# Cache attention: three pairs of PSUM banks, latents turned three steps ahead, square sums two steps behind, another order

## The chip, the cores and the metric

The kernel runs on one core of a Trainium2 chip: TensorE (PE; its weight loads are listed as PEld), VectorE (DVE), ScalarE (ACT) and GpSimd (POOL) work side by side, each in the order of its own queue, and wait for each other by semaphores. SyncE (SP) and GpSimd issue DMAs. Data lies in SBUF; matmuls write to PSUM, which has 8 banks of 512 float32 columns on 128 partitions. The metric is device time in microseconds, the median of several executions.

## The reference

One inference step of a decoder with two layers, for a prompt (1,024 tokens) and 8 samples of 4 new tokens. Each layer has a pooling mixer, a convolution mixer and an attention with a low-rank latent; only the last is touched. For the samples it runs over 8,192 past tokens of each, held in pages of latents and rotary keys:

```
    def step(carry, pt):
        m, lsum, acc = carry
        lat = cache_latent[layer, pt]
        krp = cache_krope[layer, pt]
        kn = key_nope(lat, w_uk, kn_g)
        s = attn_scores(qn, qr, kn, krp)
        m_new = jnp.maximum(m, jnp.max(s, axis=-1))
        corr = jnp.exp(m - m_new)
        p = jnp.exp(s - m_new[..., None])
        lsum = lsum * corr + jnp.sum(p, axis=-1)
        acc = acc * corr[..., None] + jnp.einsum('bhqk,bkc->bhqc', p, lat.astype(jnp.float32))
        return (m_new, lsum, acc), None
```

`key_nope` is the root-mean-square norm of `lat @ w_uk` for each head, `attn_scores` the scaled sum of `qn` with `kn` and `qr` with `krp`. There are 4 heads, 64 key dimensions without position, 32 rotary ones, latents of 128 and 4 queries for each sample. The prompt's own causal attention and the projections are computed as well.

## The kernel before

Each layer runs through a stage of input projections, a **cache stage** (`sample_attn`, L471), a **prompt stage** (`prompt_attn`, L790) that also finishes the cache attention (`finish`, L732), and output projections. In the cache and prompt stages the order of the instructions is the order in which the code is written; the stages around them are ordered by a scheduler.

The cache stage treats the past in 16 units `u` (half a sample's pages each, 4,096 tokens), a unit in 8 steps `q`; `tau` counts all 128 steps. One step covers 4 blocks of 128 tokens:

- `T` (L509): VectorE turns the latents of a step into `lT` (three buffers). The loop calls `T(tau + 2)` at the end of step `tau`.
- `K` (L519): TensorE multiplies two blocks of `lT` with `WK`, which holds `w_uk` in 256 columns and the sample's folded queries in 16 more, into a pair of PSUM banks `kproj`; each product is two MATMUL records of 272 columns. ScalarE squares the 256 columns into `sq`. `nope` (L535): ScalarE copies the 16 score columns. There are two `K` in a step, so 8 records, and two pairs of banks (`ps2`, tag `kp`) that take turns.
- `tree` (L539): GpSimd adds the two halves of the squares (`t32`). `red` (L544): VectorE sums these to `ms`, one step behind.

What belongs to a whole unit is spread over the steps of the next one: `lnexp` (ScalarE) and `newton` (VectorE) make the reciprocal root `rs`, `scale` (GpSimd) multiplies the scores with it, `rope` (TensorE) computes the rotary part of the scores from turned rotary keys (`krT`, VectorE) into `ropesc`, `addrope` (VectorE) adds it, `colmax`, `maxT` and `bcast` find the maximum over the tokens (the PSUM tile is `pm`, the two transposes run on TensorE), `expo` subtracts it, `expo_act` (ScalarE) takes the exponential into `p`, `rowsum` (VectorE) sums, `pv` (TensorE) multiplies `p` with the latents into `po`, and `pvend` (VectorE) copies `po` to `O`. In the kernel before `krT` and `rope` stand in the unit itself, at steps 2 and 5, and 6 and 7. Three gathers fetch data with indirect DMAs that GpSimd issues: `gather_c` (latents as `T` wants them, `latc`, two units ahead, step 6), `gather_n` (latents as `pv` wants them, `lat`, step 2) and `gather_kr` (rotary keys, step 7). `ada_step` (L618) computes, in layer 0 and every second unit, modulation vectors for later (`adaps`, `adapt`; seven times).

PSUM is one pool of eight banks for the whole program: two pairs `kp`, two single banks `tr`, one `rp`, one `mi` (`psr`, `psm`; `adaps`, `po`, `pm`). `ropesc` lies in `tr`. What is left after the last unit (`tail`, L696) is a generator that the prompt stage advances between its own tiles.

Of the kernel before, what the change touches and what calls it, by code (L numbers as in the profile page):

```python
# [9 lines left out]
F32 = mybir.dt.float32  # L10
# [37 lines left out]
def _build(nc, tc, a, ctx):  # L48
# [5 lines left out]
    pp = ctx.enter_context(tc.tile_pool(name="pp", bufs=2, space=PSUM))  # L54
# [7 lines left out]

    def ps2(name):
        return pp.tile([128, 2, 512], F32, tag="kp", name=name)

    def ps1(name):
        return pp.tile([128, 512], F32, tag="tr", name=name)

    def psr(name):
        return pp.tile([128, 512], F32, tag="rp", name=name, bufs=1)  # L70

    def psm(name):
        return pp.tile([128, 512], F32, tag="mi", name=name, bufs=1)

    def f(ap):
        return ap.bitcast(F32)
# [27 lines left out]
    def sub(out, x, y, e=None):  # L104
        tt(out, x, y, ALU.subtract, e)

    def split(h, lo, src, e=None):
        s.copy(h, src)  # L108
        sub(lo, src, f(h), e)

# [360 lines left out]
    def sample_attn(l, keep, pool, warm):  # L471
# [6 lines left out]
        krs = []  # L478
# [30 lines left out]
        def T(tau):  # L509
            if tau >= NU * NSTEP:  # L510
                return
            h, q = H[tau // NSTEP], tau % NSTEP
            h.lT = getattr(h, "lT", {})
            h.lT[q] = pool.tile([128, 512], F32, tag="lT", name="lT", bufs=3)
            v.transpose(h.lT[q], h.latc[:, 512 * q:512 * q + 512])  # L515
            if q == NSTEP - 1:
                h.latc = None

        def K(h, q, j):  # L519
            if q == 0 and j == 0:  # L520
                h.nope = keep.tile([128, 32, NH, NT], F32, tag="nope", name="nope", bufs=2)
                h.ms = keep.tile([128, 32, NH], F32, tag="ms", name="ms", bufs=2)
            if j == 0:
                h.sq = pool.tile([128, 4, 256], F32, tag="sq", name="sq", bufs=2)
# [14 lines left out]
        def tree(h, q):  # L539
            sv = h.sq.rearrange("p n (h x d) -> p (n h) x d", h=NH, x=2)  # L540
            h.t32 = pool.tile([128, 16, 32], F32, tag="t32", name="t32", bufs=2)
            add(h.t32, sv[:, :, 0, :], sv[:, :, 1, :], g)

        def red(h, q):  # L544
            v.tensor_reduce(h.ms[:, 4 * q:4 * q + 4, :].rearrange("p n (h o) -> p (n h) o", o=1), h.t32, AX.X, ALU.add)  # L545
# [95 lines left out]
        T(1)  # L641
        new_wk(1)
        for i in range(2):
            v.memset(pbuf[i][:, 512:528], 0.0)
        for tau in range(NSTEP * NU):
            u, q = divmod(tau, NSTEP)
            h, pu = H[u], u - 1
            hp, hpp = H.get(pu), H.get(u - 2)
            kp = K(h, q, 0)
            nope(h, q, 0, kp)  # L650
            if tau:
                red(H[(tau - 1) // NSTEP], (tau - 1) % NSTEP)
            if hp is not None:
                if q == 1:
# [10 lines left out]
            T(tau + 2)  # L665
            if hp is not None:
                if q == 0:
                    lnexp(hp)
                elif q == 1:
                    scale(hp)  # L670
                elif q == 5:
                    maxT(hp, pu)
                elif q == 6:
                    bcast(hp, pu)
                    expo(hp, pu)
                elif q == 7:
                    expo_act(hp, pu)
            if q == 0:
                if hpp is not None:
# [3 lines left out]
            elif q == 2:  # L683
                gather_n(u)
                krT(h, 0)
            elif q == 5:
                krT(h, 1)
            elif q >= 6:
                rope(h, q - 6)
                (gather_c if q == 6 else gather_kr)(u + 2)  # L690
# [5 lines left out]
        def tail():  # L696
            u = NU - 1
            h, hp = H[u], H[u - 1]
            red(h, NSTEP - 1)
            krs.clear()  # L700
            lnexp(h)
            rowsum(hp, u - 1)
# [87 lines left out]
    def prompt_attn(l, mixM, mixA):  # L790
# [164 lines left out]
        with tc.tile_pool(name=f"sa{l}", bufs=1, reuse_waits="tile") as pool:  # L955
            sample = sample_attn(l, keep, pool, warm)
        with tc.tile_pool(name=f"pa{l}", bufs=1, reuse_waits="tile") as pool:
# [714 lines left out]
```

## Time and profile before

| | |
|---|---|
| median of 3 runs | 1657.57 us (1655.13 to 1658.05) |
| the profiled execution | 1656.43 us, its span 1654.7 us |
| TensorE busy | 1580.0 us (95%) |
| VectorE, ScalarE, GpSimd busy | 1079.6, 798.5, 745.5 us (65%, 48%, 45%) |
| costliest groups | `kproj` matmuls 525.9 us, ScalarE's `sq` 305.6 us, GpSimd's `t` 325.5 us |
| moved by DMA | 254.48 MB |

The busy time of an engine is an average over stages that have different limits, and a matmul's end is modelled, so that TensorE's share says little about how close it is to its pace. The starts of matmuls tell more. In the trace an idle time stands in brackets, with the instruction that ended it.

### The profile page before, as it was taken

The numbers are of one execution on the slowest core, as the hardware profiler recorded it, in microseconds if no ns is written. First come the engines' busy times: TensorE is split into PE (matmuls) and PEld (weight loads), VectorE is DVE, ScalarE is ACT, GpSimd is POOL, SyncE is SP. The second block draws the span as 40 slices with busy tenths as digits, with TensorE's granted clock in tenths as the row PEclk, the third lists the DMA queues.
The fourth block names the chain that finished last, engine by engine and source line by source line (L and its number), as shares of the span: only waits on it lengthen the run. The fifth ranks groups of instructions, "written<-read, shape, count | busy, mean of one in ns | idle before, by whom it ended". The sixth has DMA issues, their size and how long they took to land.

```text
span 1654.7 us, 28034 instructions
## 1 busy us (share of the span) xinstructions
PE 1580.0 (95%) x10576; PEld 1367.6 (83%) x10576; DVE 1079.6 (65%) x2131; ACT 798.5 (48%) x1935; POOL 745.5 (45%) x594
## 2 busy tenths in 40 slices
PE   4899999999999999999989999999999999999999
PEld 2799999877777777889969999997777777779999
DVE  7747754577777777783377477555777777776622
ACT  4434444355555556583245344434555555566600
POOL 3301221366666667364443012124666666665520
PEclk8999999999999999999999999999999999999999
DMA  9101331676666673214422112326565555531142
GB/s 374 54 31 63 78 65 65 204 281 271 267 264 261 266 287 154 65 45 146 174 81 68 42 57 72 77 58 238 229 230 229 228 225 226 207 116 51 54 167 79
DMA packets 79557, 254.48 MB, mean 154 GB/s; under 512 B 25472, under 2 KB 49088, under 8 KB 69184
## 3 DMA queue, kind: packets, MB, share of 16 engines
q0 software_dynamic: 13824, 151.00, 23.9%
q1 hardware_dynamic: 65600, 101.69, 18.9%
q8 instruction: 85, 1.39, 0.3%
q14 instruction: 48, 0.39, 0.1%
HBM read 231.87 MB, written 20.80 MB: 153 GB/s over the span
## 4 chain that ended last, share of the span: by engine, by line
PE 79%; DVE 9%; POOL 5%; ACT 3%; issue 3%; DMA 1%; SPq 0%; DVEq 0%; ACTq 0%; POOLq 0%
PE kproj L531 23%; POOL t L96 4%; PE ropesc L557 3%; PE po L608 3%; PE outa L188 2%; PE outa L190 2%; PE outa L186 2%; PE PTp L156 2%; ACT sq L93 2%; PE rawps L206 2%; PE rawps L204 2%; PE rawps L205 2%; PE pvo L204 1%; PE outb L190 1%; PE outb L186 1%
## 5 line engine op out<-in xcount | busy, mean ns | idle before, releaser
L531 PE MATMUL kproj<-WK,lT 128*128 128x272 f32 x2048 | 525.9, 405 | 26.1 <-DVE lT L515 16.3
L531 PEld LDWEIGHTS kproj<-WK,lT 128*128 128x128 f32 x2048 | 368.0, 190 | 151.1 <-ACT nope L537 58.8
L93 ACT ACTIVATE sq<-kproj 128x512 f32<-128x512 f32 x512 | 305.6, 597 | 305.4 <-PE kproj L531 304.6
L96 POOL TENSOR_TENSOR t<-sq 128x512 f32<-128x512 f32 x256 | 325.5, 1272 | 224.1 <-ACT nope L537 222.0
L545 DVE TENSOR_REDUCE ms<-t 128x16 f32<-128x512 f32 x256 | 173.1, 676 | 156.9 <-POOL t L96 156.6
L96 POOL TENSOR_TENSOR wt<-wraw,wt 128x1024 fp32r<-128x1024 f32 x44 | 106.9, 2432 | 313.6 <-ACT wt L108 309.5
L515 DVE STREAM_TRANSPOSE lT<-latc 128x512 f32<-128x512 f32 x256 | 179.2, 700 | 0.3 <-issue 0.3
L108 ACT CAST wt<-wraw 128x1024 fp32r<-128x1024 f32 x44 | 46.7, 1064 | 124.5 <-PE outb L190 80.1
L537 ACT COPY nope<-kproj 128x32 f32<-128x32 f32 x512 | 92.4, 180 | 0.0
L96 POOL TENSOR_TENSOR kn<-raw,ones 128x128 f32<-128x128 f32 x18 | 12.2, 676 | 163.3 <-DVE raw L96 88.2
L1342 PE MATMUL zma<-hT,wt 128*128 128x352 f32 x192 | 50.6, 368 | 25.8 <-ACT hT L1122 18.7
L557 PEld LDWEIGHTS ropesc<-BD,krT 128*128 128x128 f32 x512 | 64.8, 191 | 3.5
L557 PE MATMUL ropesc<-BD,krT 128*128 128x64 f32 x512 | 67.2, 274 | 0.0
L865 DVE TENSOR_REDUCE pmx<-sc 128x1 f32<-128x128 f32 (+3 forms) x64 | 48.0, 750 | 27.1 <-PE pvo L156 21.7
L1342 PEld LDWEIGHTS zma<-hT,wt 128*128 128x128 f32 x192 | 37.0, 215 | 32.8 <-ACT hT L1122 21.5
L608 PE MATMUL po<-lat,p 128*32 128x128 f32 x2048 | 62.5, 274 | 0.0
L608 PEld LDWEIGHTS po<-lat,p 128*32 128x32 f32 x2048 | 53.9, 110 | 10.3 <-ACT nope L537 10.0
L908 ACT CAST PT<-PTp 128x512 fp32r<-128x512 f32 (+2 forms) x96 | 42.8, 481 | 40.1 <-PE PTp L156 39.5
L96 DVE TENSOR_TENSOR PT<-PTp,PT 128x512 fp32r<-128x512 f32 (+2 forms) x96 | 50.2, 550 | 16.6 <-ACT PT L908 15.6
L96 POOL TENSOR_TENSOR qkT<-src,qkT 96x512 fp32r<-96x512 f32 x32 | 40.9, 1280 | 28.0 <-ACT qkT L811 27.6
L206 PE MATMUL rawps<-wqh,hT 128*128 128x416 f32 x144 | 50.9, 354 | 0.0
L93 ACT ACTIVATE P<-sc,pmx 128x128 f32<-128x128 f32 (+3 forms) x64 | 47.9, 748 | 6.0 <-DVE pmx L865 5.4
(452 smaller groups left out, 3828.1 us busy)
## 6 DMA issues: line engine op xcount, KB each, us to landing
wada<-in_w_ada SPq DMA_DIRECT2D x11, 2048.0 KB, 9.5
wraw<-in_w_in SPq DMA_DIRECT2D x32, 512.0 KB, 3.8
wraw<-in_w_out SPq DMA_DIRECT2D x14, 512.0 KB, 5.2
qscr<-qkm SPq DMA_DIRECT2D x32, 192.0 KB, 2.1
xo<-in_xT SPq DMA_DIRECT2D x8, 528.0 KB, 4.9
xscr<-xn SPq DMA_DIRECT2D x8, 528.0 KB, 3.0
xo<-xscr SPq DMA_DIRECT2D x8, 528.0 KB, 4.8
vscr<-Vm SPq DMA_DIRECT2D x16, 256.0 KB, 2.2
```

The lines of the kernel that those rows point to most:

```text
L93: s.activation(out, in_, func, **k)
L96: (e or v).tensor_tensor(out, x, y, op)
L186: te.matmul(outs[n], wt[:, 0, k, :], hi[:, n * CH:(n + 1) * CH], start=(k == 0), stop=False)
L190: te.matmul(outs[n], wt[:, 1, k, :], hi[:, n * CH:(n + 1) * CH], start=False, stop=(k == 7))
L206: te.matmul(out, ll, rh, start=False, stop=stop)
L515: v.transpose(h.lT[q], h.latc[:, 512 * q:512 * q + 512])
L531: te.matmul(kp[:, i, 0:KPC], lT[:, sl], wk, start=True, stop=True)
L537: s.copy(h.nope[:, t0:t0 + 2].rearrange("p n h t -> p n (h t)"), kp[:, :, 256:KPC])
L545: v.tensor_reduce(h.ms[:, 4 * q:4 * q + 4, :].rearrange("p n (h o) -> p (n h) o", o=1), h.t32, AX.X, ALU.add)
L557: te.matmul(h.pr[:, o:o + 64], h.krT[c][:, 128 * k:128 * k + 128], BD[:, h.b, :], start=True, stop=True)
L608: te.matmul(h.po[32 * j:32 * j + 32, 0:128], p[:, 16 * t:16 * t + 32], h.lat[:, t * 128:(t + 1) * 128], start=(q == 0), stop=(q == 7))
L1342: te.matmul(o, zmw[j][:, i // 2, k, :], (lo if i == 1 else hi)[:, c], start=(k == 0 and i == 0), stop=(k == 7 and i == 1))
```

## The change

- `banks(stage)` closes the PSUM pool and opens another. In the cache stage it has three pairs `kp` and no `tr` in use, in all other stages two pairs as before. `ropesc` goes from `tr` to the single bank `mi` (in the last unit to `rp`).
- `lT` has four buffers, `sq` and `t32` three (they had two), `nope` three.
- `T(tau + 3)` stands at the head of step `tau`; before, `T(tau + 2)` stood at its end.
- `red` sums the squares of two steps ago, from a list; before, of one step ago.
- The unit's work is spread anew: `krT` at steps 0 and 1 of the next unit, `newton` and `scale` at 2, `lnexp` at 1, `rope` at 2 and 3, `addrope` at 4, `colmax` at 5, `maxT` at 6, `bcast` and `expo` at 7; one unit later `expo_act` at 0, `rowsum` and `pv` at 3, `pvend` at 4. `gather_n` and `gather_c` both stand at step 5. The tail has two square sums, an exponential and two rope groups more.

```
+    def banks(stage):
+
+        psum.close()
+        pools.append((psum.enter_context(tc.tile_pool(name=f"pp{len(pools)}", bufs=1, space=PSUM, reuse_waits="tile")),
+                      {"cache": 3, "main": 2}[stage]))
...
-            h.lT[q] = pool.tile([128, 512], F32, tag="lT", name="lT", bufs=3)
+            h.lT[q] = pool.tile([128, 512], F32, tag="lT", name="lT", bufs=4)
...
+            halves.append((h, q, t32))
+
+        def red():
+            h, q, t32 = halves.pop(0)
...
-                h.pr = ps1("ropesc")
+                h.pr = (psr if h is H.get(NU - 1) else psm)("ropesc")
...
+            T(tau + 3)
             kp = K(h, q, 0)
             nope(h, q, 0, kp)
-            if tau:
-                red(H[(tau - 1) // NSTEP], (tau - 1) % NSTEP)
+            if tau > 1:
+                red()
             if hp is not None:
-                if q == 1:
+                if q < 2:
+                    krT(hp, q)
+                elif q == 2:
                     newton(hp)
-                elif q == 3:
+                elif q == 4:
                     addrope(hp)
-                elif q == 4:
+                elif q == 5:
                     colmax(hp)
-            if hpp is not None and q == 0:
-                rowsum(hpp, u - 2)
             kp = K(h, q, 1)
             tree(h, q)
             nope(h, q, 1, kp)
-            T(tau + 2)
...
+            if hpp is not None:
+                if q == 0:
+                    expo_act(hpp, u - 2)
+                elif q == 3:
+                    rowsum(hpp, u - 2)
                     for i in range(8):
                         pv(hpp, u - 2, i)
+                elif q == 4:
                     pvend(hpp, u - 2)
...
+            if q == 5:
                 gather_n(u)
+                gather_c(u + 2)
```

How the order stands at the three places that matter, in layer 1. First **TensorE**, one unit of the cache stage, from one `po` to the next, before (`kproj` rows are products, four rows of the program to a step; `pm<-ident,mx` is the transpose of the maximum, `pm<-ident,M` the broadcast):

```order
L608 MATMUL po<-lat_8_12386,p_10753 32x128 x32
L531 MATMUL kproj<-WK_90,lT 128x272 x20
L156 MATMUL pm<-ident,mx 16x128
L531 MATMUL kproj<-WK_90,lT 128x272 x4
L589 MATMUL pm<-ident,M 128x16
L557 MATMUL ropesc<-BD,krT 128x64 x4
L531 MATMUL kproj<-WK_90,lT 128x272 x4
L557 MATMUL ropesc<-BD,krT 128x64 x4
L531 MATMUL kproj<-WK_90,lT 128x272 x4
L608 MATMUL po<-lat_9_12587,p_10754 32x128 x32
```

And after:

```order
L620 MATMUL po<-lat_8_12450,p_10765 32x128 x32
L541 MATMUL kproj<-WK_90,lT 128x272 x12
L166 MATMUL pm<-ident,mx 16x128
L541 MATMUL kproj<-WK_90,lT 128x272 x4
L601 MATMUL pm<-ident,M 128x16
L541 MATMUL kproj<-WK_90,lT 128x272 x12
L569 MATMUL ropesc<-BD,krT 128x64 x4
L541 MATMUL kproj<-WK_90,lT 128x272 x4
L569 MATMUL ropesc<-BD,krT 128x64 x4
L620 MATMUL po<-lat_9_12652,p_10766 32x128 x32
```

The rows are the same ones; `po` follows the second rope group directly, and the maximum comes three steps behind `po` where it came five steps behind it.

**VectorE**, around the maximum of a unit (`lT` is a turned latent tile, `ms<-t` a square sum, `mx` the maximum per column), before:

```order
L96 TENSOR_TENSOR nope<-nope,ropesc 128x512
L515 STREAM_TRANSPOSE lT<-latc_10_12469 128x512
L545 TENSOR_REDUCE ms<-t_12805 128x16
L581 TENSOR_REDUCE mx<-nope 128x16
L515 STREAM_TRANSPOSE lT<-latc_10_12469 128x512
L545 TENSOR_REDUCE ms<-t_12823 128x16
L515 STREAM_TRANSPOSE lT<-latc_10_12469 128x512
L586 TENSOR_REDUCE M<-pm 16x1
```

And after:

```order
L104 TENSOR_TENSOR nope<-nope,ropesc 128x512
L624 COPY O<-po 128x128
L525 STREAM_TRANSPOSE lT<-latc_11_12654 128x512
L557 TENSOR_REDUCE ms<-t_12776 128x16
L593 TENSOR_REDUCE mx<-nope 128x16
L525 STREAM_TRANSPOSE lT<-latc_11_12654 128x512
L557 TENSOR_REDUCE ms<-t_12831 128x16
L598 TENSOR_REDUCE M<-pm 16x1
```

The transpose of a step now stands ahead of its square sum and its maximum, and the first transpose behind `O` is the first that reads the following unit's latents.

**GpSimd**, the gathers of a unit among its trees (`t`), before:

```order
L482 DMA lat_9_12587<-in_lat,idx_87 128x4096
L96 TENSOR_TENSOR t_12603<-sq 128x512
L96 TENSOR_TENSOR t_12621<-sq 128x512
L96 TENSOR_TENSOR t_12638<-sq 128x512
L96 TENSOR_TENSOR t_12659<-sq 128x512
L482 DMA latc_11_12671<-in_latc,idx_87 128x4096
```

And after:

```order
L104 TENSOR_TENSOR nope<-nope,rs 128x512
L104 TENSOR_TENSOR t_12574<-sq 128x512
L104 TENSOR_TENSOR t_12629<-sq 128x512
L104 TENSOR_TENSOR t_12649<-sq 128x512
L492 DMA lat_9_12652<-in_lat,idx_87 128x4096
L492 DMA latc_11_12654<-in_latc,idx_87 128x4096
```

Four trees stood between the two large gathers; now none does.

## Rows read from the trace of the kernel before

**Rows 1.** The page, part 4: shares of the chain that ended last, by engine.

```profile
PE 79%; DVE 9%; POOL 5%; ACT 3%; issue 3%; DMA 1%; SPq 0%; DVEq 0%; ACTq 0%; POOLq 0%
```

**Rows 2.** The tile `kproj`, TensorE alone, layers 0 and 1: ns min/median/max, first and last start.

```profile
L531 PE MATMUL kproj<-WK,lT x1024: 392/392/657, 319.5 to 659.7; 128*128 128x272 f32 x171
...
L531 PE MATMUL kproj<-WK,lT x1024: 392/392/661, 1131.7 to 1463.3; 128*128 128x272 f32 x171
```

**Rows 3.** Windows: us, busy time of PE, PEld, DVE, ACT, POOL, granted clock, DMA share, GB/s.

```profile
319.50:330.00 10.50, 10.45 (x36) 7.39 (x37) 5.26 (x12) 5.39 (x16) 4.45 (x4) 0.84 0.43 183
...
1200.00:1300.00 100.00, 96.26 (x714) 72.74 (x712) 76.00 (x136) 56.98 (x169) 68.45 (x59) 1.00 0.59 226
```

**Rows 4.** Timeline of TensorE, one unit of layer 1: start us, us, instruction, idle before.

```profile
1298.02 1.96 PE L608 MATMUL po<-lat,p 128*32 128x128 f32 x64
1299.90 8.12 PE L531 MATMUL kproj<-WK,lT 128*128 128x272 f32 x32
1308.34 2.07 PE L531 MATMUL kproj<-WK,lT 128*128 128x272 f32 x8 [0.32 <-DVE lT L515]
1310.40 0.28 PE L156 MATMUL pm<-ident,mx 128*16 128x128 f32 x1
1311.11 2.07 PE L531 MATMUL kproj<-WK,lT 128*128 128x272 f32 x8 [0.43 <-ACT sq L93]
1313.11 0.23 PE L589 MATMUL pm<-ident,M 16*128 16x16 f32 x1
1313.27 1.10 PE L557 MATMUL ropesc<-BD,krT 128*128 128x64 f32 x8
1314.21 2.05 PE L531 MATMUL kproj<-WK,lT 128*128 128x272 f32 x8
1316.10 1.00 PE L557 MATMUL ropesc<-BD,krT 128*128 128x64 f32 x8
1316.94 2.05 PE L531 MATMUL kproj<-WK,lT 128*128 128x272 f32 x8
1318.92 1.96 PE L608 MATMUL po<-lat,p 128*32 128x128 f32 x64
```

**Rows 5.** Timeline of TensorE, layer 0, a unit with modulation work.

```profile
435.97 1.92 PE L225 MATMUL adaps<-wada,cTt 128*32 128x512 f32 x16
437.83 2.10 PE L531 MATMUL kproj<-WK,lT 128*128 128x272 f32 x8
...
442.96 0.61 PE L156 MATMUL adapt<-ident,adamg 128*128 128x128 f32 x4
443.41 2.00 PE L531 MATMUL kproj<-WK,lT 128*128 128x272 f32 x8
445.24 1.00 PE L557 MATMUL ropesc<-BD,krT 128*128 128x64 f32 x8
```

**Rows 6.** Timeline of the weight loads (PEld), the unit of rows 4.

```profile
1301.91 1.67 PEld L531 LDWEIGHTS kproj<-WK,lT 128*128 128x128 f32 x8 [0.34 <-ACT nope L537]
1303.92 1.67 PEld L531 LDWEIGHTS kproj<-WK,lT 128*128 128x128 f32 x8 [0.34 <-ACT nope L537]
```

**Rows 7.** Timeline of ScalarE, the same unit: the first pair of one step.

```profile
1303.19 0.60 ACT L93 ACTIVATE sq<-kproj 128x512 f32<-128x512 f32 x1 [0.48 <-PE kproj L531]
1303.69 0.18 ACT L537 COPY nope<-kproj 128x32 f32<-128x32 f32 x1
```

**Rows 8.** Timeline of VectorE, the same unit, around the column maximum.

```profile
1309.32 1.03 DVE L581 TENSOR_REDUCE mx<-nope 128x16 f32<-128x512 f32 x1
1310.25 0.71 DVE L515 STREAM_TRANSPOSE lT<-latc 128x512 f32<-128x512 f32 x1
```

**Rows 9.** DMA issues (median us to landing); GpSimd's timeline; a window of two us.

```profile
latc<-in_latc,idx POOLq DMA_INDIRECT x32, 8.3
...
1315.30 0.95 POOL L482 DMA_INDIRECT latc<-in_latc,idx  x1
...
1269.00:1271.00 2.00, 1.76 (x8) 1.44 (x8) 2.00 (x6) 0.77 (x4) 1.28 (x1) 1.00 0.98 418
```

More of the change, by code (lines that the diff above doesn't have):

```diff
@@ L53, in _build @@
     big = ctx.enter_context(tc.tile_pool(name="big", bufs=8))
-    pp = ctx.enter_context(tc.tile_pool(name="pp", bufs=2, space=PSUM))
+    psum = ctx.enter_context(ExitStack())
+    pools = []
     dp = ctx.enter_context(tc.tile_pool(name="dp", bufs=1, space=DRAM))
@@ L61, in slot_r @@
         return big.tile([128, 4, TOK], F32R, tag="B", name=name)
+    def banks(stage):
+        psum.close()
+        pools.append((psum.enter_context(tc.tile_pool(name=f"pp{len(pools)}", bufs=1, space=PSUM, reuse_waits="tile")),
+                      {"cache": 3, "main": 2}[stage]))
     def ps2(name):
-        return pp.tile([128, 2, 512], F32, tag="kp", name=name)
+        pp, n = pools[-1]
+        return pp.tile([128, 2, 512], F32, tag="kp", name=name, bufs=n)
     def ps1(name):
-        return pp.tile([128, 512], F32, tag="tr", name=name)
+        return pools[-1][0].tile([128, 512], F32, tag="tr", name=name, bufs=2)
     def psr(name):
-        return pp.tile([128, 512], F32, tag="rp", name=name, bufs=1)
+        return pools[-1][0].tile([128, 512], F32, tag="rp", name=name)
     def psm(name):
-        return pp.tile([128, 512], F32, tag="mi", name=name, bufs=1)
+        return pools[-1][0].tile([128, 512], F32, tag="mi", name=name)
     def f(ap):
@@ L109, in split @@
         sub(lo, src, f(h), e)
+    banks("main")
     cpk = cp.tile([128, sum(CPK.values())], F32, name="cpk")
@@ L477, in sample_attn @@
         H = {}
-        krs = []
+        krs, halves = [], []
         def rows(u, dst, src):
@@ L520, in K @@
             if q == 0 and j == 0:
-                h.nope = keep.tile([128, 32, NH, NT], F32, tag="nope", name="nope", bufs=2)
+                h.nope = keep.tile([128, 32, NH, NT], F32, tag="nope", name="nope", bufs=3)
                 h.ms = keep.tile([128, 32, NH], F32, tag="ms", name="ms", bufs=2)
             if j == 0:
-                h.sq = pool.tile([128, 4, 256], F32, tag="sq", name="sq", bufs=2)
+                h.sq = pool.tile([128, 4, 256], F32, tag="sq", name="sq", bufs=3)
             wk = WK[h.b % 2]
@@ L540, in tree @@
             sv = h.sq.rearrange("p n (h x d) -> p (n h) x d", h=NH, x=2)
[L541 to L545, printed above, removed]
+            t32 = pool.tile([128, 16, 32], F32, tag="t32", name="t32", bufs=3)
+            add(t32, sv[:, :, 0, :], sv[:, :, 1, :], g)
+            halves.append((h, q, t32))
+        def red():
+            h, q, t32 = halves.pop(0)
+            v.tensor_reduce(h.ms[:, 4 * q:4 * q + 4, :].rearrange("p n (h o) -> p (n h) o", o=1), t32, AX.X, ALU.add)
         def krT(h, c):
@@ L641, in sample_attn @@
         T(1)
+        T(2)
         new_wk(1)
@@ L664, in sample_attn @@
             nope(h, q, 1, kp)
-            T(tau + 2)
             if hp is not None:
-                if q == 0:
+                if q == 1:
                     lnexp(hp)
-                elif q == 1:
-                    scale(hp)
-                elif q == 5:
+                elif q in (2, 3):
+                    rope(hp, q - 2)
+                    if q == 2:
+                        scale(hp)
+                elif q == 6:
                     maxT(hp, pu)
-                elif q == 6:
+                elif q == 7:
                     bcast(hp, pu)
                     expo(hp, pu)
[L676 to L679, printed above, removed]
+            if hpp is not None:
[3 more added lines that the diff above has]
+                    rowsum(hpp, u - 2)
                     for i in range(8):
                         pv(hpp, u - 2, i)
+                elif q == 4:
                     pvend(hpp, u - 2)
-            elif q == 2:
+                    hpp = None
+            if q == 5:
                 gather_n(u)
[L685 to L690, printed above, removed]
+                gather_c(u + 2)
+            elif q == 7:
+                gather_kr(u + 2)
+            if u == NU - 1 and q in (4, 6):
+                krT(h, q // 2 - 2)
             ada_step(u, q)
@@ L698, in tail @@
             h, hp = H[u], H[u - 1]
-            red(h, NSTEP - 1)
+            red()
+            red()
             krs.clear()
+            expo_act(hp, u - 1)
             lnexp(h)
+            rope(h, 0)
+            rope(h, 1)
             rowsum(hp, u - 1)
@@ L955, in prompt_attn @@
         with tc.tile_pool(name=f"sa{l}", bufs=1, reuse_waits="tile") as pool:
+            banks("cache")
             sample = sample_attn(l, keep, pool, warm)
+            banks("main")
         with tc.tile_pool(name=f"pa{l}", bufs=1, reuse_waits="tile") as pool:
```

## The prediction

> **What bounds the kernel now.** I read first the shares of the chain that ended last, then the two stretches in which the cache attention runs, then one unit of it on each engine. The chain lies on TensorE for 79% [rows 1], so a gain has to be time that TensorE stands still. The diff touches the cache stage alone, and that runs twice: its first and last key products start at 319.5 and 659.7 us, and at 1131.7 and 1463.3 us [rows 2]. That is 340.2 + 331.6 = 671.8 us of the profiled execution's own 1656.43 us (1654.7 us of it the span); the median of the runs is 1657.57, 1.14 more, and I add that at the end.
>
> In such a stretch TensorE counts as busy for 96.26 of 100 us, VectorE for 76, GpSimd for 68 and ScalarE for 57, at granted clock 1.00 [rows 3], the 2.4 GHz level. The busy figure hides the loss, because a matmul's end is modelled. Starts show it: in layer 1 one unit, from one `po` to the next, takes 1318.92 - 1298.02 = 20.90 us [rows 4]. In it stand 8 steps of 8 `kproj` matmuls. Where nothing holds them, 8 take 445.24 - 443.41 = 1.83 us [rows 5], or 1316.10 - 1314.21 = 1.89 behind a rope group [rows 4]. The four steps behind `po` start 1299.90 and the fifth 1308.34, so 2.1 us each. Two waits do this. Weight loads of plain steps stand 0.34 us until ScalarE's `nope` copy has emptied a bank pair [rows 6]: from a step's first load at 1301.91 to the end of its first pair's copy at 1303.69 + 0.18 pass 1.96 us [rows 6, 7], and with two pairs the banks are wanted again after 1.83. Later in the unit the latents are late: [rows 4] show 0.32 us on `lT` at 1308.34, and the step behind the column maximum starts 0.71 us after the `pm` transpose, since VectorE turned the next latents only at 1310.25, behind the maximum [rows 8], and ScalarE then followed late.
>
> **The change, part by part.** *Three bank pairs.* A pair is wanted again after 3 x 0.92 = 2.75 us instead of 1.83, against the 1.96 it takes; 0.8 us of room for each pair. ScalarE needs 0.60 + 0.18 us for a pair [rows 7] that comes every 0.92, and 57% of 20.90 = 11.9 us in a unit [rows 3], so it keeps up. The rsqrt and the exponential (which now stand behind the second product pair of steps 1 and 0) fit into that room. The 0.34 us wait goes; what is next late in a plain step is nothing, and it runs at TensorE's own 1.83 to 1.89 us. I take 1.86.
>
> *Latents three steps ahead, at the head of a step.* VectorE's transpose now waits only for the products of the step before the current one, and TensorE wants its result three steps on, some 5.6 us for a 0.71 us instruction. The waits at 1308.34 and 1311.11 go. Behind a waiting transpose stand, on VectorE, the square sum and the unit's own instruction. VectorE's 76% of 20.90 us is 15.9 us in a unit, less than what TensorE will need, so it stays in step.
>
> *Square sums two steps behind, three buffers of squares and halves.* VectorE no longer waits for GpSimd in the step; that wait cost nothing while TensorE was late, and now keeps VectorE ahead. Count of instructions: the same.
>
> *Order.* Key rotations, rope products and everything behind them go one to three steps later; `po` follows the second rope group directly. TensorE's own work is unchanged. A unit without modulation work is then 8 x 1.86 = 14.88, two rope groups of 0.84 and 0.94 (1.78), `po` 1.88 (1299.90 - 1298.02), the small broadcast 0.16 (1313.27 - 1313.11) and the `pm` transpose, which never stands unhindered in [rows 4], taken like the broadcast, 0.16 (bounds 0.1 and 0.71): **18.86 us, 2.0 less than 20.90**. In layer 0 seven units have also 437.83 - 435.97 = 1.86 for `adaps` and 443.41 - 442.96 = 0.45 for `adapt` [rows 5]: 21.17. `adaps` now takes the bank that `po` held until VectorE copies `O`; between stands a whole product step of 1.86 us for a copy that follows `po` at once, so nothing; without that cover some 0.5 us, 7 times.
>
> *GpSimd's gathers.* `lat` moves from step 2 to step 5 and `latc` from 6 to 5, behind each other on one queue, each an issue of 0.95 us. So the tree of that step is followed by 1.9 us of issues where TensorE's step takes 1.86; GpSimd falls back some 1.7 us and wins 0.6 per step back, and the square sums read two steps later. A gather lands 8.3 us after its issue (median of 32) [rows 9]. It is 128 x 4096 x 4 bytes = 2.10 MB; the engines moved 418 GB/s in a full stretch [rows 9], so a second one behind it takes 5.0 us more: an estimate of 13.3 us from the first issue, which is some 2.2 us after the end of the step's products (1315.30 against 1313.11 [rows 9, 4]). The first latents of the gathered unit are turned at step 5 of the next unit, 18.86 - 1.86 = 17.0 us after those products. So they land 1.5 us early, and TensorE notices only another 1.3 us later, because between that transpose and `pm` lie 2 steps (3.7 us) for 2.4 us of VectorE's work (0.7 transpose, 0.7 sum, 1.03 maximum [rows 8]). Cost nothing; the cover is 2.8 us.
>
> The Trainium skill speaks against that: its page DMA: Bandwidth & Descriptors (Where 436 GB/s comes from) states about 358 GB/s as what HBM gives one core. By it the second gather takes 5.9 us and the cover shrinks by 0.9, still above zero. The 418 GB/s of the row is above that figure, so I keep the row.
>
> *The stages' ends.* Rope of the last unit (1.78 us) goes behind the loop, where before one group of 0.84 stood behind the last products; the first scores may wait for a bank that the last products used; banks change hands per tile. Plus 1.5 us per layer; bounds 0 (the prompt's start may have gaps to take it) and 3.
>
> **The sum.** Layer 1: unit 0 is products alone, 14.88; unit 1 has rope, `pm` and broadcast, 16.98; units 2 to 14 are 13 x 18.86 = 245.2; unit 15 to its last product start, 18.5. That is 295.5, plus a slow beginning as before: in the first 10.5 us of layer 0's stage the granted clock is 0.84 and only 36 matmuls start, for which 8.2 us would do at 0.229 each [rows 3]; about 2 of it remain. 297.5 against 331.6: 34.1 less. Layer 0: 14.88 + 19.3 + 7 x 18.86 + 6 x 21.17 + 18.5 + 2 = 313.7 against 340.2: 26.5 less. Together 60.6, less 3 for the ends: 57.6. 1656.43 - 57.6 = 1598.8, and on the median **1600 us**. With 1.83 for every product step and no cost at the ends it is 1589; with 1.89, `pm` at 0.71 and 3 us at each end 1627.
>
> **The rivals.**
> *Half of the gain goes to a new wait.* VectorE's queue now holds, in steps 4 to 7, four instructions that wait for TensorE in order (the rope addition, `O`, the maximum over `pm`, the subtraction), and a late one delays the next transpose and the maximum that TensorE's `pm` needs. Today the waits that come from there are 0.32 us at 1308.34, 0.2 ahead of `pm` (1310.40 against 1308.34 + 1.83) and 0.6 behind it, 1.1 in a unit [rows 4]. If they stay, 30 units x 1.1 = 33 us: 1633. For it: VectorE will be busy 15.9 of 18.9 us. Against it: the maximum has 2.8 us of room by the count above.
>
> *The pair of gathers is late: slower.* If the two land not 13.3 but 20 us after the first issue, the transpose of step 5 waits beyond its cover by 20 - 16.1 = 3.9 us in each of units 2 to 15 of both layers, 28 x 3.9 = 109 us: 1709. From 16.1 us the gain shrinks, at some 18.2 it is gone. For it: in the trace no two such gathers are under way together. Against it: `krs` follows `latc` today by 3 us in that queue, and the stretch of [rows 9] shows the engines at 0.98 without a pause.
>
> *The change does nothing.* If the bank wait were only ScalarE's pace seen from TensorE, a third pair would fill and the wait return: 1657. ScalarE's 0.78 us for a pair against 0.92 says no. The Trainium skill has such a case, in TensorE: Matmul & The Clock Gate (HAM oscillation — how this bites in real kernels): PSUM double-buffering gave one matmul kernel no further gain, 125.5 against 126.6 us. The page puts that kernel's trouble down to waits for DMA; here [rows 6] name ScalarE's copy as what ends the wait.
>
> **How the numbers follow.** Forecast, 1588 to 1617: 0.66. Half the gain lost, to 1634: 0.17. Slower by the gathers: 0.08. Nothing: 0.05. Better than 1588: 0.04. The range 1588 to 1634 leaves out 0.17. A measurement of this kernel tells about 0.2% (3.3 us) from no change. Faster 0.87, same 0.05, slower 0.08.
>
> **What would show it.** In the changed profile: plain product steps 1.83 to 1.89 us apart with no wait for `nope` in front of their weight loads; units 18.9 us in layer 1 and 21.2 with modulation; the key products from first to last some 297 and 314 us; no wait of TensorE for `lT`; `latc` landing some 13 us after the issue of `lat`; the granted clock 1.00 as before. I am wrong if VectorE's transposes wait for `latc`, if `pm` still waits for the maximum, or if the plain steps stay at 2.0 us.

## The result, and the profile after

The changed kernel takes 1605.16 us (median of 4 runs, 1603.93 to 1606.35) against 1657.09 for the kernel before beside it: a ratio of 0.9688, interval 0.9671 to 0.9705, 3.1% faster. The forecast was 1600, its range 1588 to 1634. The profiled execution took 1606.35 us, its span is 1604.6.

The two stages are where the prediction put them. First the shares of the chain that ended last, by engine (79% on TensorE before [rows 1]); then the tile `kproj` in layers 0 and 1 (first and last start behind the comma); then 100 us of layer 1 (columns as in [rows 3]):

```profile
PE 87%; DVE 6%; DMA 2%; issue 2%; ACT 1%; POOL 1%; SPq 0%; DVEq 0%; POOLq 0%; ACTq 0%
```

```profile
L541 PE MATMUL kproj<-WK,lT x1024: 392/392/497, 320.8 to 634.5; 128*128 128x272 f32 x171
...
L541 PE MATMUL kproj<-WK,lT x1024: 392/392/497, 1111.0 to 1408.1; 128*128 128x272 f32 x171
```

```profile
1180.00:1280.00 100.00, 100.00 (x755) 82.94 (x754) 90.40 (x150) 62.10 (x187) 74.65 (x65) 1.00 0.63 253
```

The stages take 313.7 and 297.1 us (340.2 and 331.6 in [rows 2]; forecast 313.7 and 297.5), 61.0 less together. The whole profiled run gained 50.1. The missing 10.9 lie outside: 1.3 ahead of the first stage (320.8 against 319.5), 4.5 between the stages (476.5 against 472.0) and 5.1 behind the second (196.5 against 191.4). The 1.3 is no work of the change: the order there is the same, and from 140 to 150 and from 150 to 160 us the granted clock reads 0.92 and 0.91 where the trace of before has 1.00; the first key product of the traces here starts anywhere from 319.3 to 323.1 us.

One unit of layer 1 on TensorE (the window ends inside the last `po`), and, behind the dots, three steps of its weight loads, to be held against [rows 4] and [rows 6]:

```profile
1209.44 1.95 PE L620 MATMUL po<-lat,p 128*32 128x128 f32 x64
1211.33 5.77 PE L541 MATMUL kproj<-WK,lT 128*128 128x272 f32 x24
1216.93 0.27 PE L166 MATMUL pm<-ident,mx 128*16 128x128 f32 x1
1217.04 2.00 PE L541 MATMUL kproj<-WK,lT 128*128 128x272 f32 x8
1218.97 0.22 PE L601 MATMUL pm<-ident,M 16*128 16x16 f32 x1
1219.13 5.77 PE L541 MATMUL kproj<-WK,lT 128*128 128x272 f32 x24
1224.73 1.00 PE L569 MATMUL ropesc<-BD,krT 128*128 128x64 f32 x8
1225.57 2.05 PE L541 MATMUL kproj<-WK,lT 128*128 128x272 f32 x8
1227.46 1.00 PE L569 MATMUL ropesc<-BD,krT 128*128 128x64 f32 x8
1228.39 0.32 PE L620 MATMUL po<-lat,p 128*32 128x128 f32 x4
...
1219.12 5.34 PEld L541 LDWEIGHTS kproj<-WK,lT 128*128 128x128 f32 x24
```

From `po` to `po` 18.95 us: the eight steps 5.60 + 1.93 + 5.60 + 1.89 = 15.02, rope 0.84 + 0.93, `po` 1.89, `pm` 0.11, the small broadcast 0.16. No row has an idle time in front, and the loads no longer wait for `nope`.

### The profile page after: what moved, and what is told of

The parts are those of the page before. It is cut to its first block, busy times and chain, and to the rows that moved or that the text cites. A ratio compares the mean times of both kernels' runs of the same rounds, so it can differ in the third digit from the quotient of the medians.

```text
span 1604.6 us, 28029 instructions
## 1 busy us (share of the span) xinstructions
PE 1547.2 (96%) x10576; PEld 1386.7 (86%) x10576; DVE 1122.6 (70%) x2131; ACT 790.4 (49%) x1935; POOL 743.8 (46%) x594
## 4 chain that ended last, share of the span: by engine, by line
PE 87%; DVE 6%; DMA 2%; issue 2%; ACT 1%; POOL 1%; SPq 0%; DVEq 0%; POOLq 0%; ACTq 0%
PE kproj L541 29%; PE po L620 4%; PE ropesc L569 3%; PE outa L198 2%; PE outa L200 2%; PE outa L196 2%; PE PTp L166 2%; PE rawps L216 2%; PE rawps L214 2%; PE rawps L215 2%; PE pvo L214 1%; DMA src<-qscr 1%; PE outb L200 1%; PE outb L196 1%; PE outb L198 1%
## 5 line engine op out<-in xcount | busy, mean ns | idle before, releaser
L541 PE MATMUL kproj<-WK,lT 128*128 128x272 f32 x2048 | 497.5, 397 | 3.9 <-DVE lT L525 3.9
L541 PEld LDWEIGHTS kproj<-WK,lT 128*128 128x128 f32 x2048 | 378.9, 190 | 90.0 <-issue 15.9
L525 DVE STREAM_TRANSPOSE lT<-latc 128x512 f32<-128x512 f32 x256 | 177.4, 694 | 35.7 <-PE kproj L541 31.9
L557 DVE TENSOR_REDUCE ms<-t 128x16 f32<-128x512 f32 x256 | 167.0, 652 | 10.8 <-POOL t L104 10.5
L104 DVE TENSOR_TENSOR PT<-PTp,PT 128x512 fp32r<-128x512 f32 (+2 forms) x96 | 50.2, 551 | 21.8 <-ACT PT L929 20.8
L104 POOL TENSOR_TENSOR nope<-nope,rs 128x512 f32<-128x512 f32 x32 | 35.2, 1100 | 35.2 <-DVE rs L581 35.2
```

Source lines behind the costliest of these rows:

```text
L104: (e or v).tensor_tensor(out, x, y, op)
```

## The experiments

Ratios are to the kernel before, run beside each. The old order is that of the kernel before; "lag" is square sums two steps behind, "lead" latents three steps ahead.

| kernel | pairs | order | lag | lead | us | ratio, interval |
|---|---|---|---|---|---|---|
| before | 2 | old | no | no | 1657.1 | 1 |
| e_bk3 | 3 | old | no | no | 1659.7 | 1.0012, 1.0002 to 1.0021 |
| e_lag | 3 | old | yes | yes | 1647.1 | 0.993, 0.991 to 0.995 |
| e_order | 2 | new | no | no | 1675.7 | 1.0104, 1.0084 to 1.0125 |
| e_twotlate | 2 | new | yes | no | 1628.4 | 0.9827, 0.9800 to 0.9855 |
| e_two | 2 | new | yes | yes | 1628.0 | 0.9818, 0.9801 to 0.9834 |
| e_red1 | 3 | new | no | yes | 1614.1 | 0.9731, 0.9711 to 0.9751 |
| e_tlate | 3 | new | yes | no | 1607.0 | 0.9689, 0.9673 to 0.9705 |
| after | 3 | new | yes | yes | 1605.2 | 0.9688, 0.9671 to 0.9705 |

### Parts taken away from the changed kernel

Two pairs (e_two):

```diff
-                      {"cache": 3, "main": 2}[stage]))
+                      {"cache": 2, "main": 2}[stage]))
```

> The changed kernel with two pairs of banks for the key products in the cache stage instead of three (the freed banks stay empty); order, latents three steps ahead and square sums two steps behind stay. Theory 1 (two separate waits, as the prediction has it): a pair is wanted again after 1.83 us and takes 1.96, so a plain step takes 1.96 to 2.1 instead of 1.83, 8 x 0.13 to 0.27 = 1.0 to 2.2 us per unit, 32 units: 1637 to 1675, middle about 1645; weight loads wait for the nope copy again. Theory 2 (the latents alone held TensorE, the third pair only adds slack): 1604 to 1612, and the wait for nope stays away.

1628.0, between the two theories. The wait for `nope` is back in front of the weight loads. Their group in the view of lines (busy, mean ns, idle before it), in the changed kernel and in e_two:

```profile
L541 PEld LDWEIGHTS kproj<-WK,lT 128*128 128x128 f32 x2048 | 378.9, 190 | 90.0 <-issue 15.9
```

```profile
L541 PEld LDWEIGHTS kproj<-WK,lT 128*128 128x128 f32 x2048 | 367.0, 190 | 130.9 <-ACT nope L547 50.0 <-issue 15.9
```

A plain step starts every 2.01 us instead of 1.83 (from ScalarE's first square of each step), which is the turnaround of two pairs of banks, and the unit is 19.70 instead of 18.94: 0.76 x 32 = 24 us, against 23 us lost.

Late latents (e_tlate):

```diff
-        T(2)
...
-            T(tau + 3)
             kp = K(h, q, 0)
...
             nope(h, q, 1, kp)
+            T(tau + 2)
```

> The changed kernel with the latents turned two steps ahead at the end of a step, as before the change, with three pairs of banks and all the rest as changed. Theory 1 (two separate waits): what the prediction priced for the late latents comes back, about 1.1 us per unit, 30 units: 1630 to 1645; TensorE waits for lT behind the column maximum again. Theory 2 (three pairs give ScalarE room, so that a transpose two steps ahead is early enough): 1604 to 1612, no wait for lT.

Theory 2: 1607.0, and no difference in the total that can be told from the changed kernel. TensorE waits 4.6 us for `lT` in the whole run by name. The trace does not say that the lead is worth nothing, though. A unit takes 19.10 us instead of 18.94, because the third step behind the small broadcast starts late:

```profile
1227.25 1.67 PEld L541 LDWEIGHTS kproj<-WK,lT 128*128 128x128 f32 x8 [0.32 <-issue]
```

The two stages are 3.6 and 4.4 us longer than in the changed kernel, and the stretches between and behind them 3.6 and 5.4 us shorter (472.9 and 191.1 us). Part of the 4.4 is a slow beginning, at granted clock 0.51 in the first 3 us. As to the shorter stretches, ScalarE waits there only 1.75 and 1.05 us for a load of which the section on the stages' ends tells (3.06 and 3.96 in the changed kernel). In the sum the two hide each other. With two pairs the late latents make no difference (e_twotlate):

> The changed kernel with two pairs of banks and latents two steps ahead at the end of a step; square sums stay two steps behind. Two pairs alone gave 1628, late latents alone 1607, both with sums one step behind 1676. Theory 1 (the lead of the latents is a cover that is needed once ScalarE empties banks late): 1645 to 1676, TensorE waits for lT again. Theory 2 (the lag of the sums is what the two pairs need): 1628 to 1635.

1628.4: theory 2, and the unit is 19.70 us as in e_two. The kernel e_order, told below, differs from it in the lag alone and takes 47 us more.

Sums one step behind (e_red1):

```diff
-            if tau > 1:
+            if tau:
                 red()
```

> The changed kernel with the square sums one step behind instead of two. Theory 1 (VectorE has 3 us of slack in a unit and the latents three steps of lead, so its wait for GpSimd's halves stays hidden): 1604 to 1608, while VectorE waits some 100 us or more for GpSimd again. Theory 2 (that wait delays the maximum and with it pm): 1612 to 1640, TensorE waits in front of pm.

1614.1, 9 us more than the changed kernel, near the low end of theory 2: VectorE waits 111.4 us for GpSimd's halves (10.5 in the changed kernel), and a unit goes from 18.94 to 19.27.

### Parts added to the kernel before

Three pairs alone (e_bk3):

```diff
-    pp = ctx.enter_context(tc.tile_pool(name="pp", bufs=2, space=PSUM))
...
+    def banks(stage):
...
-                h.pr = ps1("ropesc")
+                h.pr = psr("ropesc")
...
-                h.po = (psm if u == NU - 2 else psr)("po")
+                h.po = (psr if u == NU - 1 else psm)("po")
...
-                ada_end(*ada[c], A.mg, psr("adapt"))
+                ada_end(*ada[c], A.mg, psm("adapt"))
```

> The kernel before with three pairs of banks for the key products in the cache stage and nothing else of the change: latents two steps ahead at the end of a step, square sums one step behind, the old order of a unit. Rope products take the bank of po, po and adapt that of pm, and the last unit's rope stands behind the loop, since the single banks for them are gone. Theory 1 (the third pair has a price of its own, about the 23 us that taking it away costs in the changed kernel): 1630 to 1640. Theory 2 (the late latents behind the column maximum hide it in the old order): 1648 to 1658. Theory 3 (the pairs are nearly the whole change): 1605 to 1620.

1659.7: theory 2, or a little worse; it gave nothing at all. (The stage of layer 0 is 4.4 us longer than before: `adapt` waits 0.8 us in each of seven units for the bank that it has to share there. The units without it are as long as before in both layers.) The rows say why. TensorE in a unit of e_bk3, and VectorE's transpose of the latents for the step at 1312.21:

```profile
1303.76 7.64 PE L541 MATMUL kproj<-WK,lT 128*128 128x272 f32 x32
1312.21 2.07 PE L541 MATMUL kproj<-WK,lT 128*128 128x272 f32 x8 [0.81 <-ACT nope L547]
1314.25 0.28 PE L166 MATMUL pm<-ident,mx 128*16 128x128 f32 x1
1314.95 2.07 PE L541 MATMUL kproj<-WK,lT 128*128 128x272 f32 x8 [0.43 <-ACT sq L101]
...
1311.36 0.70 DVE L525 STREAM_TRANSPOSE lT<-latc 128x512 f32<-128x512 f32 x1
```

The four plain steps take 7.64 us instead of 8.12 [rows 4], and the next stands 0.81 us instead of 0.32: gained and given back on the spot. The idle time is put down to ScalarE's last `nope` copy, but with three pairs the bank that this step wants was emptied two copies earlier (by 1310.24); what came late is the latents, turned by 1312.06. The unit is 20.89 us, as before. VectorE's square sums in the traces of before, e_bk3, e_order and after (busy, mean ns, idle before them):

```profile
L545 DVE TENSOR_REDUCE ms<-t 128x16 f32<-128x512 f32 x256 | 173.1, 676 | 156.9 <-POOL t L96 156.6
```

```profile
L555 DVE TENSOR_REDUCE ms<-t 128x16 f32<-128x512 f32 x256 | 173.1, 676 | 156.6 <-POOL t L104 156.3
```

```profile
L557 DVE TENSOR_REDUCE ms<-t 128x16 f32<-128x512 f32 x256 | 171.7, 671 | 146.3 <-POOL t L104 145.5
```

```profile
L557 DVE TENSOR_REDUCE ms<-t 128x16 f32<-128x512 f32 x256 | 167.0, 652 | 10.8 <-POOL t L104 10.5
```

156.6 us over 32 units is 4.9 in a unit; with 76% busy of 20.90, that is 15.9 [rows 3], VectorE's time is 20.8: all of the unit. So VectorE waits for GpSimd and hardly ever for TensorE (0.4 us in a unit, for `po`), though TensorE is the engine that counts as nearly full. Its transposes show it, before and after:

```profile
L515 DVE STREAM_TRANSPOSE lT<-latc 128x512 f32<-128x512 f32 x256 | 179.2, 700 | 0.3 <-issue 0.3
```

```profile
L525 DVE STREAM_TRANSPOSE lT<-latc 128x512 f32<-128x512 f32 x256 | 177.4, 694 | 35.7 <-PE kproj L541 31.9
```

In the changed kernel VectorE is ahead of TensorE and waits for its products (31.9 us). The old unit was a loop: VectorE turns latents, TensorE multiplies, ScalarE squares, GpSimd adds the halves, and VectorE waits for the sums with the next latents behind in its queue.

The new order alone (e_order: two pairs, and the edits of e_tlate and e_red1):

> The changed kernel with two pairs of banks, latents two steps ahead at the end of a step and square sums one step behind, so that of the change the new order of a unit (with the gathers' places and the tail) is left. Theory 1 (the parts add up: pairs 23 us, latents 2, sums 0 to 5, so order the remaining 22 to 27): 1628 to 1637. Theory 2 (latents and sums matter as soon as ScalarE empties the banks late, so that they cover each other's loss): 1640 to 1657.

1675.7, above even theory 2: slower than the kernel before. TensorE waits 42.1 us for `lT` (16.3 before). The parts do not add up: in the new order the lag is worth 47 us with two pairs and late latents, and 9 with three pairs and early ones.

Lag, lead and three pairs in the old order (e_lag; on top of e_bk3, besides the changed lines of `T`, `tree` and `red`):

```diff
-            if tau:
-                red(H[(tau - 1) // NSTEP], (tau - 1) % NSTEP)
+            if tau > 1:
+                red()
...
-                if q == 1:
+                if q == 2:
                     newton(hp)
```

> The kernel before with three pairs of banks, latents three steps ahead at the head of a step and square sums two steps behind, but the old order of a unit and the old places of the gathers; only the rsqrt, the Newton step and the scaling, which need the last square sum, go one step later. Three pairs alone left the unit at 20.89 us: VectorE there is busy for 15.9 us of it and waits some 5 us in front of square sums for GpSimd's halves, with the next latents queued behind. Theory 1 (that loop of VectorE, TensorE, ScalarE and GpSimd sets the old unit, and lead and lag open it): a unit of 18.9 to 19.9 us, total 1605 to 1630. Theory 2 (the new order is what opens it): 1640 to 1660.

1647.1: theory 2. VectorE's wait for GpSimd is gone (0.4 us), so the loop is open, but TensorE now stands in front of `pm`. The units take 20.40 and 21.26 us in turn; in the longer ones it also stands 0.77 us in front of the small broadcast. TensorE and VectorE of e_lag:

```profile
1305.38 0.28 PE L166 MATMUL pm<-ident,mx 128*16 128x128 f32 x1 [1.18 <-DVE mx L593]
...
1315.32 0.29 DVE L624 COPY O<-po 128x128 f32<-128x128 f32 x1 [2.38 <-PE po L620]
```

With the last sum a step later, the chain from it over rsqrt, scaling and the addition of the rope scores to the maximum ends behind the place that the old order gives to `pm`. I first took VectorE's wait for `po` for the cause and moved that copy one step on (e_lagO):

```diff
                         pv(hpp, u - 2, i)
-                    pvend(hpp, u - 2)
+            elif q == 1:
+                if hpp is not None:
+                    pvend(hpp, u - 2)
```

> The kernel with three pairs, lead and lag in the old order of a unit (1647), with one piece of the new order added: VectorE's copy of po stands at the end of step 1 instead of step 0, right behind the product that it waits for. In 1647 VectorE waits 2.38 us for po in that copy, with the next latents, sums and in the end the column maximum behind it, and TensorE stands 1.18 us in front of pm. Theory 1 (an in-order wait of VectorE for TensorE is what the new order takes away): the wait for po goes, the wait before pm with it, 1 us or more per unit: 1605 to 1625. Theory 2 (VectorE had the time to wait; the rest of the order, rope and maximum three steps earlier than in the new one, holds TensorE): 1640 to 1648.

1647.8 (0.994, 0.9923 to 0.9957): theory 1 fell. The wait for `po` shrank from 2.38 to 0.63, `pm` came as late as ever:

```profile
1305.39 0.28 PE L166 MATMUL pm<-ident,mx 128*16 128x128 f32 x1 [1.18 <-DVE mx L593]
```

That the later `pm` is the part of the new order that matters is read from these rows; no run moved it by itself. The trace of e_lag shows a rival. In the chain that ends at `pm`, two of VectorE's instructions of the Newton step take longer than the 0.28 and 0.29 us of the trace of before, each until 0.14 us behind the end of one of GpSimd's additions (the last section tells of this). VectorE, then GpSimd:

```profile
1318.66 0.74 DVE L104 TENSOR_TENSOR rs<-ta 128x128 f32<-128x128 f32 x1
...
1319.90 1.33 DVE L581 SCALAR_TENSOR_TENSOR rs<-rs,ta 128x128 f32<-128x128 f32 x1
...
1319.82 1.27 POOL L104 TENSOR_TENSOR t<-sq 128x512 f32<-128x512 f32 x1 [0.56 <-ACT nope L547]
```

They lose 1.5 us together, so also in the median of the 32 units, and from there to the maximum VectorE has no idle time; TensorE's wait for `pm` is 1.18. So the old order may have been short of room for this delay only, where the new one has room for a longer one. No run tells the two apart.

### The cover of the pair of gathers (e_pair7)

```diff
-            if q == 5:
+            if u == NU - 1 and q == 5:
                 gather_n(u)
-                gather_c(u + 2)
-            elif q == 7:
+            if q == 7:
+                if u < NU - 1:
+                    gather_n(u)
+                gather_c(u + 2)
                 gather_kr(u + 2)
```

> The changed kernel with the pair of gathers (lat, latc) moved from step 5 to step 7 of a unit, in front of the one for the rotations (last unit as changed). This measures the cover of the pair. By the prediction's count (latents land 1.5 us early, TensorE notices 1.3 us after that, cover 2.8 us) the two steps of 3.8 to 4.1 us cost 1.0 to 1.3 us in each of 28 units: about 1633 to 1642, and VectorE's transposes wait for the gather. By the trace of the changed kernel (the gather issued at 1218.67 lands at 1231.6, the transpose of the next unit's step 5 is due at 1234.5, so 2.9 us early, cover about 4.2 us) it costs nothing or up to 0.3 us a unit: 1604 to 1614.

1659.2 (1.0013, 1.0002 to 1.0024): two steps later, and the whole gain is gone, 54 us or 1.9 in each of 28 units. Both expectations fell short. VectorE waits 43.8 us in 24 transposes for `latc`, and `pm` with it:

```profile
1227.25 0.71 DVE L525 STREAM_TRANSPOSE lT<-latc 128x512 f32<-128x512 f32 x1 [1.15 <-DMA latc<-in_latc,idx]
...
1229.51 0.28 PE L166 MATMUL pm<-ident,mx 128*16 128x128 f32 x1 [0.78 <-DVE mx L593]
```

In the changed kernel the cover reads thus: GpSimd issues the first gather at 1217.39, the second lands at 1231.6 (12.9 us behind its own issue at 1218.67), 14.2 us on. The transpose that needs it starts at 1232.41 (the second expectation had counted from the next one, 1234.5). That is 0.8 us early, and the maximum behind it ends at 1234.62, 1.3 us ahead of `pm` (1216.93 + 18.95 = 1235.88). The cover is 2.1 us. Steps 5 and 6 take 3.8; 3.8 less 2.1 is 1.7 in a unit, and 1.9 were lost.

```profile
1217.39 0.97 POOL L492 DMA_INDIRECT lat<-in_lat,idx  x1
1218.67 0.94 POOL L492 DMA_INDIRECT latc<-in_latc,idx  x1 [0.30 <-issue]
...
1232.41 0.71 DVE L525 STREAM_TRANSPOSE lT<-latc 128x512 f32<-128x512 f32 x1 [0.36 <-PE kproj L541]
1233.05 0.64 DVE L557 TENSOR_REDUCE ms<-t 128x16 f32<-128x512 f32 x1
1233.61 1.01 DVE L593 TENSOR_REDUCE mx<-nope 128x16 f32<-128x512 f32 x1
```

### The stages' ends

Where the prompt attention begins in layer 1, ScalarE and TensorE of the changed kernel, and two windows behind:

```profile
1420.14 0.62 ACT L832 CAST qkT<-src 96x512 fp32r<-96x512 f32 x1 [3.96 <-DMA src<-qscr]
...
1421.76 0.79 PE L214 MATMUL sc<-qkT 96*128 96x512 f32 x1 [3.62 <-ACT P L101]
```

```profile
1421.70:1425.00 3.30, 3.25 (x9) 2.34 (x10) 3.17 (x6) 2.48 (x6) 2.67 (x4) 0.50 0.00 0
1425.00:1428.00 3.00, 3.00 (x14) 2.76 (x13) 1.98 (x4) 1.33 (x2) 0.52 (x1) 0.50 0.00 0
```

and the same places in the trace of before:

```profile
1471.63 0.62 ACT L811 CAST qkT<-src 96x512 fp32r<-96x512 f32 x1 [2.17 <-DMA src<-qscr]
...
1473.03 0.55 PE L156 MATMUL PTp<-ident,P 128*128 128x128 f32 x3 [1.95 <-DVE PT L96]
```

```profile
1473.00:1476.00 3.00, 2.97 (x10) 2.08 (x11) 2.97 (x5) 2.68 (x7) 2.38 (x4) 0.57 0.01 3
```

The cast of head 1 waits for its load; the exponential behind it, which TensorE needs, stands in the same queue. TensorE stands 3.62 us instead of 1.95 and then works at granted clock 0.50, the 1.2 GHz level, for over 6 us; in the trace of before a stretch of 3 us behind the gap reads 0.57. Beside it 1.9 us of rope products have moved ahead of `po` (from the last product to `po` 4.05 us, before 2.12). The load is late because the last unit's `lat`, gathered at step 5 instead of 2, is still under way. Three runs tell this cause from the rival, the banks that change hands.

The last gather at step 1 (e_lat15):

```diff
+            if u == NU - 1 and q == 1:
+                gather_n(u)
             if q == 5:
-                gather_n(u)
+                if u < NU - 1:
+                    gather_n(u)
```

> The changed kernel, with the latent rows (lat) of the last unit gathered at step 1 of that unit instead of step 5; nothing else moves. In the changed kernel the gather is issued at 633.23 and 1406.83 us, the load of head 1 behind it at 635.52 and 1409.12; the load lands 8.9 to 9.8 us after its issue (before: 3.6 to 5.2), ScalarE waits 3.06 and 3.96 us for it (before 1.24 and 2.17), TensorE stands 2.72 and 3.62 us, and the scores behind that run at half clock for some 5 us. Theory 1 (the late gather shares the transfer engines with the load): the load lands 4 to 5.5 us after its issue, ScalarE waits 0 to 1 us, TensorE under 1 us, the half-clock stretch is short or gone; 2 to 4 us per layer come back, total 1597 to 1601. Theory 2 (the gap is due to the banks that change hands, or to the rope products behind the loop): ScalarE's wait shrinks, TensorE's time at the prompt's start does not; total 1604 to 1606.

1603.1 (0.9672, 0.9656 to 0.9688). At the ends theory 1 holds in full: the load lands 3.9 and 4.3 us after its issue, ScalarE does not wait, the granted clock stays at 1.00, and the stretches outside are 471.4 and 190.4 us. The stages were 3.3 us longer each. Half of it is the edit's own: the memory that the gather fills is free only behind the last transpose of `latc` in that unit, so GpSimd stood 3.96 us in front of it, `pm` waited 1.34, and steps 5 and 6 took 1.6 us more. Most of the rest, some 1.7 us, lies in the first steps of a stage, and is no work of the edit: in the first 3 us the granted clock is 0.53 and 0.54, near the 1.2 GHz level, where the trace of the changed kernel has 1.00 in both stages. Other traces have it low too (before 0.54 and 0.57, e_qk 0.52 and 0.59).

The casts one tile later, the gather untouched (e_qk):

```diff
-                    if y < 4:
-                        qk_part(hh + 1, y, s)
+                    z = y - (hh == 0)
+                    if 0 <= z < 4:
+                        qk_part(hh + 1, z, s)
```

> The changed kernel with the casts of head 1 (and the loads of head 2 behind them) one row tile later in the prompt attention; the last gather stays at step 5. Theory 1 (the loss at the stages' ends is that the casts and exponentials behind them stand in ScalarE's queue behind the load): the load still lands some 9 us after its issue, ScalarE waits 1 to 2 us for it instead of 3 to 4, the gap of TensorE shrinks by about 2 us per layer: 1599 to 1603. Theory 2 (the gap only moves by one tile): 1604 to 1607.

1600.1 (0.9652, 0.9633 to 0.9670): theory 1. The load still lands 7.9 and 9.6 us after its issue and ScalarE waits 2.14 us for it, but the scores ahead no longer stand behind that wait.

Both, with the gather at step 4 (e_lat4qk):

> The changed kernel with two moves at the stages' ends: the last unit's latent rows are gathered at step 4 of that unit (right behind the last transpose of the latents whose memory they take; at step 1 GpSimd waited 3.96 us for that and the last steps lost 1.6 us) instead of 5, and ScalarE's and GpSimd's casts of head 1 (and with them the loads of head 2) stand one row tile later in the prompt attention. Theory 1 (the loss at the stages' ends is ScalarE's queue standing behind the load of head 1, and the half clock that follows): no wait of ScalarE for src, TensorE's gap of 2.7 and 3.6 us gone, 3 to 4 us per layer: 1597 to 1600. Theory 2 (the casts one tile later are late for head 1's scores, or the gap comes back elsewhere): 1603 to 1610.

1599.2 (0.964, 0.962 to 0.966): theory 1, and the fastest kernel here, some 6 us below the changed one; 472.1 and 191.1 us outside the stages, as before the change. Over e_qk it adds nothing that can be told.

## Why the prediction was right, and where it was not

- **The sum.** Units: forecast 18.86 us, measured 18.95; stages within 0.4 us. It held because it asked what TensorE needs when nothing holds it, and every other engine had room for that. `pm` takes 0.11 (taken 0.16), plain steps 1.83 from start to start, the eight steps 15.02 (taken 14.88), a unit with modulation 21.44 (taken 21.17). That the stages come out within 0.4 us has luck in it: the units are 1 to 2.5 us longer per layer than forecast, and the 2 us of a slow beginning, taken "as before", are missing in this trace, where the clock is high from the first product on (before, [rows 3]: 36 products in the first 10.5 us, at 0.84). In other runs the beginning was slow again (e_lat15 above). The same stretch of the changed kernel, columns as in [rows 3]:

```profile
320.80:331.00 10.20, 10.20 (x45) 8.45 (x46) 7.04 (x15) 6.65 (x20) 5.17 (x5) 1.00 0.46 193
```

- **Why the parts were priced wrongly.** The step "The 0.34 us wait goes; what is next late in a plain step is nothing" failed for the part by itself: three pairs alone moved the wait into the next step (e_bk3). So did "that wait cost nothing while TensorE was late", on VectorE's wait for GpSimd: it filled VectorE's time up to the whole old unit. The latents three steps ahead, which were to take the waits at 1308.34 and 1311.11 away (1.1 us in a unit by the prediction's count of such waits), are worth 0.16 us in a unit with three pairs and nothing with two. Lag and order, priced at nothing, open the loop together (e_order and e_lag, each with one of them, keep most of the old time), and only then is the third pair worth its 23 us. So the time was forecast from the right end state, but not for the reasons that the part-by-part prices gave.
- **The mis-sized term: the stages' ends.** 1.5 us per layer, bounds 0 and 3; measured 4.5 and 5.1. The rope products were counted; a load behind the moved gather was not: the prediction followed the moved gathers on GpSimd's queue and to their readers in the next unit, but not the last of them into the prompt stage. This is why 1605 and not 1600 came out.
- **The rivals.** *Half of the gain lost* did not come: VectorE is busy 90.4% (76% before, [rows 3]), but TensorE waits only 3.9 us for `lT` in the whole run. *Gathers late* did not come either, but the cover was 2.1 us and not 2.8, because the pair takes 14.2 us and not 13.3. The 13.3 rested on 418 GB/s of two us; ten us of the pair show 410 (the row below), and in them a third, smaller gather, issued at 1222.29, takes its share. The Trainium skill, DMA: Bandwidth & Descriptors (Where 436 GB/s comes from), gives 358 GB/s for a core's HBM; the estimate by it was 8.3 + 5.9 = 14.2. The trace agrees with that sum but not with the rate, which it exceeds for ten us, so the agreement may be chance. *The change does nothing* is not so for the whole, but for the third pair alone it is what was measured.

```profile
1221.00:1231.00 10.00, 10.00 (x108) 8.68 (x108) 9.93 (x16) 5.67 (x19) 8.14 (x7) 1.00 0.97 410
```

- **What would show it.** The named signs came, `latc` at 14.2 us instead of 13; the granted clock is 1.00 inside the stages (1180 to 1280) but not right behind them.

## What to carry to other kernels

Ask of each engine what it waits for in one period. Where an engine that is busy for only three quarters of it spends all the rest waiting for one partner, and never for the engine that is taken for the limit, it is part of a loop, and the wait that another engine shows may only be where the loop's slack surfaces. A second step of lag, another buffer and an order that fits both are then one change, not three with prices of their own. When a transfer is moved, look at what is loaded behind it at the end of the stage, and at what stands in the queue behind the instruction that waits for that load.

## What the runs showed beside it

VectorE's first operation of the Newton step, `rs<-ta`, 128 x 128 with both inputs in SBUF, takes 0.28 us in all 32 units of the trace of before, and 1.96 in the median of the changed one. First VectorE, then GpSimd of the changed kernel:

```profile
1206.24 1.96 DVE L104 TENSOR_TENSOR rs<-ta 128x128 f32<-128x128 f32 x1
...
1204.33 3.72 POOL L104 TENSOR_TENSOR t<-sq 128x512 f32<-128x512 f32 x3
```

It ends 0.15 us behind GpSimd's third addition (1208.05), having started in the second; once in each layer, beside three of them, it took 3.19. The Trainium skill, SBUF — State Buffer (Who interferes with whom), has it that a VectorE instruction with two inputs in SBUF contends with a GpSimd instruction that reads SBUF, for a pair of ports that works as an exclusive lock. The trace agrees, and shows that VectorE can also miss its turn between two additions that follow at once. In the new order this costs VectorE 1.7 us in the median unit, which TensorE does not notice; it more than makes up the step from the 15.9 us that the prediction gave VectorE to the 17.1 (90.4% of 18.95) it is busy. In e_lag the same kind of wait lies on the way to `pm`, which TensorE there does wait for.
